# Early stage of a hybrid decoder block: x turned by TensorE, GpSimd left out, and emission ordered by model clocks

## The chip, the cores and the metric

One core of one Trainium2 chip. The metric is the device time of one execution in microseconds, the median of three runs.

## The reference

A residual block on x (512 tokens, 2048 channels, float32). What the early part of the kernel computes:

```python
mod = c @ w_ada[l] + b_ada[l]
shift, scale, gate = jnp.split(mod, 3, axis=-1)
h = rmsnorm(x, norm_gain[l]) * (1.0 + scale[:, None]) + shift[:, None]
proj = h @ w_in[l]
qa, ka, va, za, qm, km, vm, om, zm, ifg, ga, gb = jnp.split(proj, offsets, axis=-1)
...
qk = jax.nn.silu(causal_depthwise_conv(jnp.concatenate([qm, km], axis=-1), conv_w[l], conv_b[l]))
...
yb = (hm * jax.nn.silu(zm)) @ w_proj_mlstm[l]
```

The rest (dilated attention, the mLSTM in chunks, the merge, the output product, the last norm) comes later in the kernel and the change doesn't touch it.

## The kernel before, in words

All products are made in float32 by three fast products (`mm3`): each operand is split into a high part (a cast to fp32r on ScalarE, L172) and a low part (the difference, a subtraction, L173), and TensorE adds high x high, high x low, low x high.

The early stage makes sixteen blocks of h, transposed: h0 to h15, each 128 channels x 512 tokens, and with each of them the products that can be made already. One turn k consists of these steps:

- **Pieces.** The modulation c @ w_ada is made on VectorE, not on TensorE: a *piece* is a 128x1024 part of w_ada (transposed on the host) times c, summed along the row (`tensor_tensor_reduce`, L338). Scale and shift of a block need two pieces each, so a turn needs four, and the stage 64. The pieces lie in a ring `y` of eight buffers of 512 KB.
- **The chain of h.** When the fourth piece is done, `modulated(k)` (L391) makes gs (VectorE, 128x1, L393), modulates the block of x on ScalarE (L396), casts it (ScalarE, L172), makes the low part (VectorE for k = 0, otherwise GpSimd, L173), and stores h to DRAM.
- **First products.** A unit `ws[k]` (128x768) holds the weights of the six blocks of 128 columns in `FIRST`; its two halves make 9 matmuls each (`first_products`, L440), which accumulate in six PSUM banks over all k.
- **Extra products.** Ten more blocks of columns (`EXTRA`) are made in five groups of k (`GROUPS`: 2, 4, 4, 4 and 2 blocks of h). `TURNS` says which of them are emitted in which turn: a product is 3 matmuls for each block of its group, two products come from one unit of `wu`. Group 0 is copied to SBUF by ScalarE (L515), the others are added to it by VectorE (L517).

Weights come through a ring `raw` of three buffers and one `more`; high and low parts lie in rings `hi` and `lo` of four. A buffer is free again when the low part of its second half has been made. Low parts of `ws` are made by VectorE, those of the extra units by GpSimd. x comes transposed from the host (`xT`); it is squared on ScalarE, summed over channels by products with a matrix of ones, and each block is multiplied by the reciprocal root on GpSimd (`normed`, L387; the first on VectorE).

The order of instructions on each engine is the order in which the program emits them, and every engine works through its own in that order. All loads are emitted on SP's queue from one list `loads`, in the order in which units were added: `load_ahead` (L193) stops at the first whose ring has no free buffer. `step` (L256) keeps three split halves ahead (`prepare`, L207), emits what was left over (`late`), and then one product. How many pieces are emitted ahead of a product is a fixed count: `next_pieces` (L434) spreads the four pieces of turn k + 1 evenly over the products of turn k, two pieces ahead (`AHEAD`).

PSUM has five banks with tag `d` and three with tag `m`. After the early stage a stage of 258-column products over `wv` begins.

Of the kernel before, what the change touches and what calls it, by code (L numbers as in the profile page):

```python
# [11 lines left out]
F32 = mybir.dt.float32  # L12
# [39 lines left out]
TURNS = {  # L52
# [51 lines left out]
@with_exitstack  # L104
def block_kernel(ctx: ExitStack, tc, xT, x, c, cst, abias, ada, ws, wu, wv, fgain, out):
    nc = tc.nc
# [70 lines left out]
    pos = [0, 0]  # L177
    stream, loads, pieces, ready, late, tasks, beside = [], [], [], [], [], [], []
    at = {"load": 0, "split": 0, "half": 0, "piece": 0, "raw": 0, "more": 0, "y": 0}

# [8 lines left out]
    def add(u):  # L189
        stream.append(u)  # L190
        loads.append(u)

    def load_ahead():  # L193
        while at["load"] < len(loads):
            u = loads[at["load"]]
            if u.ring == "any":
                u.ring = "raw" if at["raw"] < RAW or "more" not in tags else "more"
            if at[u.ring] == {"raw": RAW, "more": MORE, "y": ADA}[u.ring]:
                if u.ring == "more":
                    u.ring = "any"  # L200
                break
            if u.at_load:
                u.at_load()
            u.raw = S(u.ring)
            dma(u.raw[:, : u.width], u.src)
            at["load"] += 1
            at[u.ring] += 1  # L207

    def prepare():

        if at["split"] == len(stream):
            return False
        load_ahead()
        u = stream[at["split"]]
        if at["half"] == 0 and u.at_split:
            u.at_split()
        if u.use:
            u.use(u.raw)
        else:
            n, i = u.width // 2, at["half"]  # L220
            if u.keep:
                hi, lo = u.keep()
            else:
                hi, lo = S("hi", F32R), S("lo", F32R)
            split(u.raw[:, i * n : (i + 1) * n], hi[:, :n], lo[:, :n], u.low)
            if later and u.low is None:
                normed(later.pop(0), nc.gpsimd)
            ready.append((u.products[i], hi, lo, u.keep is None))
# [18 lines left out]
    def modulate(n):  # L247

        while at["piece"] < min(n, len(pieces)):
            load_ahead()  # L250
            u = pieces[at["piece"]]
            u.use(u.raw)
            at["piece"] += 1
            at[u.ring] -= 1

    def step():  # L256
# [28 lines left out]
    cs = const.tile([P, C_MASK], F32, name="cs")  # L285
    xt = []

# [6 lines left out]

    def load_x(n):
        for _ in range(n):
            t = S("gm")
            dma(t, xT[len(xt)])
            xt.append(t)
# [4 lines left out]
    load_x(4)  # L304
# [4 lines left out]
    load_x(12)  # L309
    mask = S("mk")  # L310
# [6 lines left out]
    bmod = const.tile([P, 3 * KD], F32, name="bmod")  # L317
    nc.vector.tensor_copy(bmod, cs[:, C_BADA : C_BADA + 3 * KD])
    nc.vector.tensor_scalar(bmod[:, KD : 2 * KD], bmod[:, KD : 2 * KD], 1.0, None, ALU.add)
    cb = []  # L320
# [7 lines left out]
    def modulation(j, k, at_load=None, ring="any", then=None):  # L328

        col = j * KD + k  # L330
        acc = []

        def use(half):
            def f(raw):
                if half == 0:
                    acc.append(small([P, 1], "acc", 4))
                dst = acc[0] if half == 0 else mods[:, col : col + 1]
                nc.vector.tensor_tensor_reduce(  # L338
                    out=raw[:, :1024], in0=raw[:, :1024], in1=cb[half][:, :1024], scale=1.0,
                    scalar=bmod[:, col : col + 1] if half == 0 else acc[0],  # L340
                    op0=ALU.mult, op1=ALU.add, accum_out=dst,
                )
                if half and then:
                    then()
            return f

        for half in range(2):
            u = Unit(ada[col * 2 + half], use=use(half), at_load=at_load if half == 0 else None, ring=ring)
            loads.append(u)
            (pieces if then or ring == "y" else stream).append(u)  # L350
# [5 lines left out]
    qm, km, szm = [None] * 8, [None] * 8, [None] * 8  # L356

    def first_norm():

        acc = S("w")  # L360
# [11 lines left out]
        rstd = acc[:, 512:]  # L372
        nc.scalar.activation(rstd, ss, AF.Sqrt, bias=eps, scale=1.0 / D)
        nc.vector.reciprocal(rstd, rstd)
        rs.append(rstd)
        normed(0, nc.vector)
        modulate(3)
        for _ in range(2):
            prepare()
        modulate(4)  # L380
        for k in range(1, 4):
            normed(k, nc.gpsimd)

    rs = []
    later = []

    def normed(k, e):  # L387
        e.tensor_tensor(xt[k], xt[k], rs[0], ALU.mult)

    def modulated(k):  # L390
        def f():  # L391
# [12 lines left out]
            if k + 4 < KD:  # L404
                later.append(k + 4)
            hh.append(a)
# [23 lines left out]

    turn = []
    AHEAD = 2

    def next_pieces():  # L434

        k, n, i = turn
        modulate(4 * (k + 1) + AHEAD + 4 * (i + 1) // n)
        turn[2] += 1

    def first_products(k, half):  # L440
        def f(hi, lo):
            if half == 0:
                modulate(4 * (k + 1) + AHEAD)
                turn[:] = [k, 2 * (1 + len(TURNS.get(k, []))), 0]
# [7 lines left out]
            next_pieces()  # L452
        return f
# [50 lines left out]
    def extra_products(g, n):  # L504
        def f(hi, lo):
            ps = PS("m")
            k0, size = GROUPS[g]
            for kk in range(size):
                s = slice(kk * P, (kk + 1) * P)
                mm3(ps, hi[:, s], lo[:, s], hh[k0 + kk], hl[k0 + kk], kk == 0, kk == size - 1, True)  # L510

            def done():
                if g == 0:
                    extra.append(S("g"))
                    nc.scalar.copy(extra[n], ps)  # L515
                else:
                    nc.vector.tensor_tensor(extra[n], extra[n], ps, ALU.add)  # L517
# [3 lines left out]
            next_pieces()  # L521
        return f
# [3 lines left out]
    for k in range(KD):  # L526
        add(
            Unit(ws[k], 768, [first_products(k, 0), first_products(k, 1)], low=None)
        )
        modulation(1, k, ring="y")  # L530
        modulation(0, k, ring="y", then=modulated(k))
        for g, n in TURNS.get(k, []):
            width = 2 * GROUPS[g][1] * P
            add(
                Unit(next(src)[:, :width], width, [extra_products(g, n), extra_products(g, n + 1)], low=nc.gpsimd)
            )
    loads[:5] = loads[1:4] + loads[:1] + loads[4:5]
    load_ahead()
# [221 lines left out]
    def pair_units():  # L760

        for d in pairs():
            for u, src in enumerate(begin("S", d[2], d[3])):
                unit = Unit(src, ring="raw")
                loads.append(unit)
                paired.append((d, u, unit))
# [761 lines left out]
```

## Time and profile before

| what | value |
|---|---|
| runs, us | 1637.99, 1634.11, 1637.28 (median 1637.28) |
| profiled execution | 1637.23 us, span 1635.4 us |
| TensorE | 1565.2 us busy, 9686 matmuls |
| VectorE | 1147.9 us busy |
| ScalarE | 704.6 us busy |
| GpSimd | 139.8 us busy, nearly all before 260 us |
| DMA | 260.01 MB, mean 159 GB/s |

In the profile TensorE's matmuls are called PE (weight loads PEld), VectorE is DVE, ScalarE is ACT, GpSimd is POOL and the queue that issues the loads is SP. "L173" is line 173 of the program; since `split` is a helper, the names of the tiles tell whose low part it is. Times in a timeline count from the start of the span. The early stage runs from the start to about 247 us.

### The profile page before, as it was taken

How to read it: one execution, taken by the hardware profiler on the slowest of the kernel's cores; microseconds unless marked ns; L12 is line 12 of the kernel's file. 1: busy time of each engine (PE TensorE's matmuls, PEld its weight loads, DVE VectorE, ACT ScalarE, POOL GpSimd, SP SyncE). 2: the span in 40 equal slices, each digit the busy share in tenths (PEclk: the TensorE clock that was granted, in tenths of full speed). 3: DMA queues.
4: the chain of work that ended last, by engine and by line, in shares of the span. 5: the costliest groups of instructions: out<-in, count | busy, mean ns of one | idle time of the engine just before them, and what ended most of it. 6: DMA issues, size and time to landing. Idle time of an engine off the chain costs nothing.

```text
span 1635.4 us, 24961 instructions
## 1 busy us (share of the span) xinstructions
PE 1565.2 (96%) x9686; PEld 1388.3 (85%) x9686; DVE 1147.9 (70%) x1933; ACT 704.6 (43%) x1189; POOL 139.8 (9%) x112
## 2 busy tenths in 40 slices
PE   3799899999999999999999999999999999999997
PEld 1576689988888888999999999999999788878887
DVE  6788867667746568888788887888896444474445
ACT  3332344335525434455454454454443843343234
POOL 2665540000000000000000000000000000000000
PEclk7999999999999999999999999999999999999999
DMA  8677735665222344344443444444444654432333
GB/s 313 241 276 273 272 113 168 223 217 179 90 94 74 104 163 159 139 152 130 142 144 124 146 145 137 144 142 132 133 161 149 216 176 137 176 105 95 125 117 129
DMA packets 93879, 260.01 MB, mean 159 GB/s; under 512 B 10424, under 2 KB 14648, under 8 KB 93760
## 3 DMA queue, kind: packets, MB, share of 16 engines
q1 hardware_dynamic: 79928, 233.24, 41.6%
q10 hardware_dynamic: 13832, 25.18, 4.4%
q8 instruction: 76, 1.25, 0.3%
q14 instruction: 43, 0.35, 0.1%
HBM read 229.02 MB, written 29.36 MB: 158 GB/s over the span
## 4 chain that ended last, share of the span: by engine, by line
PE 71%; DVE 13%; issue 6%; ACT 4%; DMA 3%; POOL 1%; SPq 0%; ACTq 0%; DVEq 0%; POOLq 0%
PE ps L280 47%; PE ps L807 23%; DVE y L338 3%; DVE lo L173 2%; ACT sh L172 2%; DVE cs L780 1%; DVE e L822 1%; DVE cs L784 1%; DVE cs L785 1%; DMA raw<-ws 1%; DVE sl L173 1%; DVE al L786 1%; DMA p<-kept 1%; DMA more<-ws 1%; ACT gm L396 1%
## 5 line engine op out<-in xcount | busy, mean ns | idle before, releaser
L173 DVE TENSOR_TENSOR lo<-raw,hi 128x512 fp32r<-128x512 f32 (+2 forms) x238 | 177.5, 751 | 172.1 <-ACT hi L172 171.7
L172 ACT CAST hi<-raw 128x512 fp32r<-128x512 f32 (+3 forms) x276 | 161.2, 596 | 277.9 <-PE ps L280 227.4
L807 PE MATMUL ps<-t,sh 128*128 128x256 f32 x1344 | 245.3, 282 | 0.0
L807 PEld LDWEIGHTS ps<-t,sh 128*128 128x128 f32 x1344 | 208.0, 190 | 0.0
L807 PE MATMUL ps<-t,sl 128*128 128x256 f32 x672 | 189.3, 282 | 0.0
L779 ACT CAST ah<-raw 128x768 fp32r<-128x768 f32 x112 | 93.6, 836 | 204.8 <-issue 105.2
L280 PE MATMUL ps<-ha,hi 128*128 128x512 f32 x384 | 126.5, 409 | 26.1 <-ACT ha L172 17.2
L173 DVE TENSOR_TENSOR sl<-cs,sh 128x1024 fp32r<-128x1024 f32 x112 | 137.3, 1226 | 16.0 <-ACT sh L172 15.7
L172 ACT CAST sh<-cs 128x1024 fp32r<-128x1024 f32 x112 | 117.6, 1050 | 67.8 <-DVE cs L785 67.4
L786 DVE TENSOR_TENSOR al<-raw,ah 128x768 fp32r<-128x768 f32 x112 | 106.9, 955 | 52.8 <-ACT ah L779 52.6
L280 PE MATMUL ps<-hi,h 128*128 128x512 f32 (+1 forms) x512 | 143.6, 366 | 0.0
L280 PE MATMUL ps<-hi,ha 128*128 128x258 f32 (+1 forms) x512 | 129.8, 339 | 0.0
L280 PE MATMUL ps<-hi,hb 128*128 128x258 f32 (+1 forms) x512 | 129.3, 339 | 0.0
L807 PEld LDWEIGHTS ps<-t,sl 128*128 128x128 f32 x672 | 127.8, 190 | 0.0
L280 PE MATMUL ps<-hb,hi 128*128 128x512 f32 x384 | 122.0, 397 | 1.6 <-POOL hb L173 1.6
L280 PEld LDWEIGHTS ps<-ha,hi 128*128 128x128 f32 x384 | 73.9, 195 | 48.3 <-ACT ha L172 19.2
L280 PEld LDWEIGHTS ps<-hi,h 128*128 128x128 f32 x512 | 91.8, 188 | 17.0
L807 PE MATMUL ps<-hb,ah 128*128 128x256 f32 x448 | 87.1, 287 | 11.5 <-DVE e L822 9.9
L280 PEld LDWEIGHTS ps<-hi,ha 128*128 128x128 f32 x512 | 87.8, 188 | 11.4 <-issue 0.4
L280 PEld LDWEIGHTS ps<-hi,hb 128*128 128x128 f32 x512 | 87.9, 188 | 10.8
L280 PE MATMUL ps<-lo,h 128*128 128x512 f32 (+1 forms) x256 | 93.9, 367 | 2.4 <-DVE lo L173 2.4
L280 PE MATMUL ps<-h,hi 128*128 128x512 f32 x286 | 89.6, 395 | 0.0
(276 smaller groups left out, 3461.8 us busy)
## 6 DMA issues: line engine op xcount, KB each, us to landing
raw<-wu SPq DMA_DIRECT2D x223, 512.0 KB, 3.6
y<-ada SPq DMA_DIRECT2D x64, 512.0 KB, 7.3
g<-kept SPq DMA_DIRECT2D x56, 256.0 KB, 3.9
kept<-e ACTq DMA_DIRECT2D x56, 256.0 KB, 2.5
raw<-ada SPq DMA_DIRECT2D x24, 512.0 KB, 3.7
more<-wu SPq DMA_DIRECT2D x16, 512.0 KB, 3.5
raw<-wv SPq DMA_DIRECT2D x12, 516.0 KB, 3.7
kept<-g ACTq DMA_DIRECT2D x20, 256.0 KB, 4.2
```

What stands on the lines that cost most here:

```text
L172: nc.scalar.copy(hi, src)
L173: (low or nc.vector).tensor_tensor(lo, src, as32(hi), ALU.subtract)
L280: nc.tensor.matmul(ps, a, b, start=first and n == 0, stop=last and n == 2)
L338: nc.vector.tensor_tensor_reduce(out=raw[:, :1024], in0=raw[:, :1024], in1=cb[half][:, :1024], scale=1.0, scalar=bmod[:, col : col + 1] if ...
L396: nc.scalar.activation(xt[k], xt[k], AF.Identity, bias=mods[:, k : k + 1], scale=gs)
L779: nc.scalar.copy(ah, r[:, HT : 4 * HT])
L780: nc.vector.tensor_tensor(two(s[:, : 2 * HT]), two(r[:, HT : 3 * HT]), r[:, :HT].unsqueeze(1).to_broadcast([P, 2, HT]), ALU.add,)
L784: nc.vector.tensor_tensor(s[:, 2 * HT : 3 * HT], s[:, :HT], r[:, 2 * HT : 3 * HT], ALU.add)
L785: nc.vector.tensor_tensor(s[:, 3 * HT :], s[:, 2 * HT : 3 * HT], r[:, 3 * HT : 4 * HT], ALU.add)
L786: nc.vector.tensor_tensor(al, r[:, HT : 4 * HT], as32(ah), ALU.subtract)
L807: nc.tensor.matmul(banks[bank][:, n * HT : (n + 1) * HT], x[:, w], y, start=count[bank] == 1, stop=count[bank] == 24 * len(BANKS[bank]),)
L822: nc.vector.tensor_tensor(v[:, 0:2, :], twice(v[:, 4, :]), two(bb), ALU.add)
```

## The change

1. **x.** The host no longer transposes it. Sixteen tiles of 128 tokens x 512 channels are loaded from `x` (`load_x(j)`, four column parts j). Squares with an accumulator give the sums along the row, ten on ScalarE and six on VectorE; root and reciprocal are of 128x4 (one value for each token). `normed(j)` scales the four tiles of part j by a value for each partition, on ScalarE (half of part 0 on VectorE). `turned(k)` transposes a block by four 128x128 transposes of TensorE into an `m` bank, and ScalarE copies it to SBUF; blocks 0 and 1 stay in PSUM until they are modulated. Blocks 0 to 3 are turned ahead of the first product, 4 to 7 in turns 0 and 1, 8 to 15 behind the products of group 0.
2. **GpSimd.** All low parts of the stage are made by VectorE.
3. **Emission.** While pieces are left (`pacing`), the program keeps model clocks of SP, DMA, ScalarE, VectorE and TensorE with fixed prices for each operation. Loads stand in two lists (`y` and `raw`), and the next load is taken from the list whose buffer is free first by these clocks. A low part is `owe`d: it is emitted (`settle`) when VectorE's model clock has passed its cast, or when the product that needs it is next. `fill` emits pieces as long as they end before a time that is worked out for the next cast or 4 us before the next product is due. `AHEAD` and `next_pieces` are gone.
4. **TURNS.** All five units of group 0 are in turn 1 (before: turns 1 to 4).

The core of the diff:

```diff
-    1: [(0, 0)], 2: [(0, 2), (0, 4)], 3: [(0, 6)], 4: [(0, 8)],
+    1: [(0, 0), (0, 2), (0, 4), (0, 6), (0, 8)],
...
+        while pacing() and not (want and want.raw is not None):
+            kinds = []
+            for kind in loads:
+                if loads[kind]:
+                    ring = loads[kind][0].ring
+                    rings = ["y"] if ring == "y" else ["raw", "more"]
+                    times = [free[r][0] for r in rings if free[r]]
+                    if times:
+                        kinds.append((min(times), kind))
+            if not kinds or (not want and min(kinds)[0] > clock["DVE"]):
...
+            if not begin_load(min(kinds)[1]):
+                break
...
+    BEGIN, LAND, LOAD = 0.45, 2.0, 1.3 / 1024
+    PIECE, CHAIN, CAST, LOW, MATMUL = 1.33, 1.65, (0.13, 0.00096), (0.15, 0.00105), 0.233
+    room = {"raw": RAW, "more": MORE, "y": ADA}
...
+    def settle(until=None):
+        while owed and (owed[0][0] <= clock["DVE"] if until is None else until in [o[1] for o in owed]):
+            t, key, cost, f = owed.pop(0)
+            clock["DVE"] = max(clock["DVE"], t) + cost
+            ready_at[key] = clock["DVE"]
+            f()
...
+    def fill(until):
+        while at["piece"] < len(pieces):
+            load_ahead()
+            settle()
+            u = pieces[at["piece"]]
+            if at["piece"] % 4 == 3 and at["piece"] // 4 not in xt:
+                break
+            if u.raw is None or max(clock["DVE"], u.there) + PIECE > until + 0.4:
+                break
+            modulate(at["piece"] + 1)
...
+        if pacing():
+            load_ahead(u)
+            n = u.width // 2
+            cast = lambda: max(clock["ACT"], ends[at["half"] + 2 * at["split"]], u.there) + CAST[0] + CAST[1] * n
+            due = clock["PE"] + sum(3 * MATMUL / P * r[4][2] for r in ready if r[4])
+            come = max(ends[at["half"] + 2 * at["split"]], u.there) + CAST[0] + CAST[1] * n
+            fill(max(come, due - 4.0))
...
+            clock["ACT"] = cast()
+            nc.scalar.copy(hi[:, :n], part)
+            def low():
+                nc.vector.tensor_tensor(lo[:, :n], part, as32(hi[:, :n]), ALU.subtract)
+                if i == 1:
+                    at[u.ring] -= 1
+                    free[u.ring].append(clock["DVE"])
...
+            owe(clock["ACT"], (u, i, n), LOW[0] + LOW[1] * n, low)
+            ready.append((u.products[i], hi, lo, True, (u, i, n)))
+            at["half"] = 1 - i
...
         pending, late[:] = list(late), []
         for f in pending:
+            fill(clock["PE"])
             f()
-        f, hi, lo, _ = ready.pop(0)
+        f, hi, lo, _, key = ready.pop(0)
+        if key:
+            settle(key)
+            clock["PE"] = max(clock["PE"], ready_at.get(key, 0.0))
         f(hi, lo)
+        if key:
+            ends.append(clock["PE"])
         pump()
...
-        ss = PS("m")
-        for k in range(KD):
-            sq = acc[:, :512] if k == 0 else S("hb")
-            nc.scalar.activation(sq, xt[k], AF.Square)
-            if k % 3 == 2 and k < KD - 2:
-                nc.tensor.matmul(ss, ones, sq, start=k == 2, stop=False)
-            elif k:
-                nc.vector.tensor_tensor(acc[:, :512], acc[:, :512], sq, ALU.add)
-        nc.tensor.matmul(ss, ones, acc[:, :512], start=False, stop=True)
...
+        for j in range(NT):
+            for t in range(NT):
+                to, junk = sums[:, t, j : j + 1], S("hb")
+                if (j * NT + t) % 8 in (2, 5, 7):
+                    nc.vector.tensor_tensor_reduce(
+                        out=junk, in0=xn[j][t], in1=xn[j][t], scale=1.0, scalar=0.0,
+                        op0=ALU.mult, op1=ALU.add, accum_out=to,
+                    )
+                else:
+                    nc.scalar.activation(junk, xn[j][t], AF.Square, accum_out=to)
...
+        nc.vector.tensor_reduce(rstd, sums, mybir.AxisListType.X, ALU.add)
+        nc.scalar.activation(rstd, rstd, AF.Sqrt, bias=eps, scale=1.0 / D)
         nc.vector.reciprocal(rstd, rstd)
...
+        normed(0, True)
+        for k in (2, 3, 0, 1):
+            turned(k)
+        clock["DVE"] = clock["ACT"] = clock["PE"] = clock["DMA"] = 5.0
+        normed(1)
         for _ in range(2):
             prepare()
         modulate(4)
...
+    def normed(j, both=False):
+        for t in range(NT):
+            r = rstd[:, t : t + 1]
+            clock["ACT"] += 0.0 if both else 0.62
+            if both and t % 2:
+                nc.vector.tensor_scalar(xn[j][t], xn[j][t], r, None, ALU.mult)
+            else:
+                nc.scalar.activation(xn[j][t], xn[j][t], AF.Copy, scale=r)
+    def turned(k):
+        ps = PS("m")
+        clock["PE"] += 0.5
+        end = clock["PE"]
+        for t in range(NT):
+            nc.tensor.transpose(ps[:, t * P : (t + 1) * P], xn[k // 4][t][:, k % 4 * P : (k % 4 + 1) * P], ident)
+        def copy():
+            xt[k] = S("hb" if k < HK else "gm")
+            clock["ACT"] = max(clock["ACT"], end) + 0.55
+            nc.scalar.copy(xt[k], ps)
+        if k < 2:
+            xt[k] = ps
+        elif k < 4:
+            copy()
+        else:
+            late.append(copy)
...
-            nc.scalar.activation(xt[k], xt[k], AF.Identity, bias=mods[:, k : k + 1], scale=gs)
+            src = xt[k]
+            if k < 2:
+                xt[k] = S("hb")
+            nc.scalar.activation(xt[k], src, AF.Identity, bias=mods[:, k : k + 1], scale=gs)
...
-            split(xt[k], a, b, nc.gpsimd if k else None)
+            nc.scalar.copy(a, xt[k])
+            clock["DVE"] += 0.15
+            clock["ACT"] = max(clock["ACT"], clock["DVE"]) + CHAIN
+            owe(clock["ACT"], k, 0.7, lambda: nc.vector.tensor_tensor(b, xt[k], as32(a), ALU.subtract))
             put(("h", k), xt[k])
...
+                modulate(4 * (k + 1))
+                settle(k)
+                clock["PE"] = max(clock["PE"], ready_at[k])
...
+            clock["PE"] += 9 * MATMUL
+            for j in {(0, 0): (4, 5), (1, 0): (6,), (1, 1): (7,)}.get((k, half), ()):
+                turned(j)
+            if (k, half) == (1, 1):
+                normed(2)
...
+            clock["PE"] += 3 * size * MATMUL
+            end = clock["PE"]
+            if g == 0 and n < 8:
+                turned(8 + n)
+            if g == 0 and n == 1:
+                normed(3)
```

## Rows read from the trace of the kernel before

**Rows 1.** Page, busy time, share of the span, instructions of each engine.
```profile
PE 1565.2 (96%) x9686; PEld 1388.3 (85%) x9686; DVE 1147.9 (70%) x1933; ACT 704.6 (43%) x1189; POOL 139.8 (9%) x112
```
**Rows 2.** Windows of TensorE, line 280: stretch, busy (matmuls), granted clock, DMA share, GB/s.
```profile
0.00:36.07 36.07, 0.00 (x1) 0.74 0.88 328
36.07:194.78 158.71, 138.97 (x546) 0.96 0.73 261
194.78:240.00 45.22, 45.22 (x194) 1.00 0.43 151
...
36.07:41.23 5.16, 5.16 (x12) 0.50 0.52 188
```
**Rows 3.** Chain of waits up to 300 us, its last piece: start, length, what.
```profile
194.78 105.31 PE ps L280 x665
```
**Rows 4.** Timeline, the first matmul of the next stage: start, length, engine, operation.
```profile
246.77 0.28 PE L280 MATMUL ps<-hi,ha 128*128 128x258 f32 x1
```
**Rows 5.** Timeline from the squares to the end of the fourth piece.
```profile
8.54 8.03 ACT L366 ACTIVATE hb<-gm 128x512 f32<-128x512 f32 x12 [0.74 <-DMA gm<-xT]
...
20.55 3.35 DVE L374 RECIPROCAL w<-w 128x512 f32<-128x512 f32 x1 [2.89 <-ACT w L373]
...
24.55 2.29 DVE L338 CUSTOM_DVE_ANT_0 y<-y,w,bmod 128x1024 f32<-128x1024 f32 x1
...
34.37 0.08 DVE L338 DVE_READ_ACCUMULATOR2_ANT mods<- 128x1 f32 x1
```
**Rows 6.** The tiles of x: durations, first and last issue; time to landing.
```profile
L154 SPq DMA_DIRECT2D gm<-xT x16: 327/399/549, 0.7 to 10.5; - x16
...
DMA to landing us min/median/max: 2.9/5.2/5.5
```
**Rows 7.** Timeline of VectorE and GpSimd around 37 us; in brackets GpSimd's idle time.
```profile
36.66 0.55 DVE L173 TENSOR_TENSOR lo<-raw,hi 128x384 fp32r<-128x384 f32 x1
37.12 1.28 DVE L338 CUSTOM_DVE_ANT_0 y<-y,w,bmod 128x1024 f32<-128x1024 f32 x1
...
42.20 0.15 DVE L393 TENSOR_TENSOR gs<-mods,cs 128x1 f32<-128x1 f32 x1
...
43.99 1.27 POOL L173 TENSOR_TENSOR ha<-gm,ha 128x512 fp32r<-128x512 f32 x1 [11.63 <-ACT ha L172]
```
**Rows 8.** Groups of VectorE up to 240 us: count, busy, mean ns, idle before.
```profile
L338 DVE CUSTOM_DVE_ANT_0 y<-y,w,bmod 128x1024 f32<-128x1024 f32 x32 | 59.2, 1850 | 0.0
L338 DVE CUSTOM_DVE_ANT_0 y<-y,w,acc 128x1024 f32<-128x1024 f32 x32 | 47.7, 1489 | 0.7
L173 DVE TENSOR_TENSOR lo<-raw,hi 128x384 fp32r<-128x384 f32 x24 | 31.1, 1302 | 22.1 <-ACT hi L172 22.1
L517 DVE TENSOR_TENSOR g<-g,ps 128x512 f32<-128x512 f32 x34 | 23.0, 678 | 11.0 <-PE ps L280 11.0
```
**Rows 9.** Groups of VectorE from 240 to 600 us.
```profile
L173 DVE TENSOR_TENSOR lo<-raw,hi 128x512 fp32r<-128x512 f32 x63 | 43.0, 688 | 36.8 <-ACT hi L172 36.7
...
L173 DVE TENSOR_TENSOR y<-y,y 128x258 fp32r<-128x258 f32 x16 | 5.7, 422 | 0.0
```
**Rows 10.** Windows, busy PE, PEld, DVE, ACT, POOL; clock, DMA share, GB/s.
```profile
60.00:80.00 20.00, 16.23 (x65) 12.14 (x64) 15.25 (x20) 9.16 (x19) 11.86 (x9) 0.97 0.86 304
...
140.00:160.00 20.00, 18.55 (x78) 14.63 (x79) 18.09 (x24) 5.16 (x9) 15.93 (x9) 1.00 0.77 259
...
36.07:194.78 158.71, 138.97 (x546) 104.70 (x546) 132.08 (x165) 50.47 (x95) 92.19 (x57) 0.96 0.73 261
```
**Rows 11.** Timeline, four transposes in a stream of matmuls later on.
```profile
424.23 0.39 PE L280 MATMUL ps<-hb,lo 128*128 128x512 f32 x1
...
424.46 0.60 PE L982 MATMUL ps<-cs,w 128*128 128x128 f32 x4
...
424.81 0.71 PE L280 MATMUL ps<-hb,hi 128*128 128x512 f32 x2
```
**Rows 12.** Waits from 36.07 to 194.78: total, times, longest.
```profile
DVE lo L173 <- ACT hi L172: 26.1, 13, 2.7
```
**Rows 13.** Waits of SP's queue, the same stretch.
```profile
SPq L154 <- DVE lo L173: 91.4, 13, 9.7
```

More of the change, by code (lines that the diff above doesn't have):

```diff
@@ L177, in block_kernel @@
     pos = [0, 0]
-    stream, loads, pieces, ready, late, tasks, beside = [], [], [], [], [], [], []
-    at = {"load": 0, "split": 0, "half": 0, "piece": 0, "raw": 0, "more": 0, "y": 0}
+    stream, loads, pieces, ready, late, tasks, beside = [], {"y": [], "raw": []}, [], [], [], [], []
+    at = {"split": 0, "half": 0, "piece": 0, "raw": 0, "more": 0, "y": 0}
     def begin(*desc):
@@ L190, in add @@
         stream.append(u)
[L191 to L200, printed above, removed]
-                break
[L202 to L207, printed above, removed]
+        loads["raw"].append(u)
@@ new lines, in begin_load @@
+    def begin_load(kind):
+        u = loads[kind][0]
+        if u.ring == "any":
+            u.ring = "raw" if at["raw"] < RAW or "more" not in tags else "more"
+        if at[u.ring] == room[u.ring]:
+            if u.ring == "more":
+                u.ring = "any"
+            return False
+        if u.at_load:
+            u.at_load()
+        u.raw = S(u.ring)
+        dma(u.raw[:, : u.width], u.src)
+        loads[kind].pop(0)
+        at[u.ring] += 1
+        if pacing():
+            clock["SP"] = max(clock["SP"], free[u.ring].pop(0)) + BEGIN
+            clock["DMA"] = max(clock["DMA"], clock["SP"] + LAND) + LOAD * u.width
+            u.there = clock["DMA"]
+        return True
@@ new lines, in load_ahead @@
+    def load_ahead(want=None):
+        while pacing() and not (want and want.raw is not None):
[8 more added lines that the diff above has]
+            if not kinds or (not want and min(kinds)[0] > clock["DVE"]):
+                break
+            if not begin_load(min(kinds)[1]):
+                break
+        if not pacing():
+            for kind in loads:
+                while loads[kind] and begin_load(kind):
+                    pass
@@ new lines, in block_kernel, with pacing @@
+    BEGIN, LAND, LOAD = 0.45, 2.0, 1.3 / 1024
+    PIECE, CHAIN, CAST, LOW, MATMUL = 1.33, 1.65, (0.13, 0.00096), (0.15, 0.00105), 0.233
+    room = {"raw": RAW, "more": MORE, "y": ADA}
+    free = {r: [0.0] * n for r, n in room.items()}
+    clock = {"SP": 0.0, "DMA": 0.0, "ACT": 0.0, "DVE": 0.0, "PE": 0.0}
+    owed, ends, ready_at = [], [0.0] * SPLIT, {}
+    def pacing():
+        return at["piece"] < len(pieces)
+    def settle(until=None):
[4 more added lines that the diff above has]
+            f()
@@ L212, in prepare @@
             return False
+        u = stream[at["split"]]
         load_ahead()
-        u = stream[at["split"]]
+        if pacing():
+            load_ahead(u)
[4 more added lines that the diff above has]
+            fill(max(come, due - 4.0))
+            hi, lo = S("hi", F32R), S("lo", F32R)
+            i = at["half"]
+            part = u.raw[:, i * n : (i + 1) * n]
+            clock["ACT"] = cast()
[8 more added lines that the diff above has]
+            at["half"] = 1 - i
+            if i == 1:
+                at["split"] += 1
+            return True
         if at["half"] == 0 and u.at_split:
@@ L225, in prepare @@
             split(u.raw[:, i * n : (i + 1) * n], hi[:, :n], lo[:, :n], u.low)
-            if later and u.low is None:
-                normed(later.pop(0), nc.gpsimd)
-            ready.append((u.products[i], hi, lo, u.keep is None))
+            ready.append((u.products[i], hi, lo, u.keep is None, None))
             at["half"] = 1 - i
@@ L249, in modulate @@
         while at["piece"] < min(n, len(pieces)):
-            load_ahead()
             u = pieces[at["piece"]]
+            load_ahead(u)
+            settle()
+            clock["DVE"] = max(clock["DVE"], u.there) + PIECE
             u.use(u.raw)
@@ L254, in modulate @@
             at[u.ring] -= 1
+            free[u.ring].append(clock["DVE"])
+            load_ahead()
     def step():
@@ L285, in block_kernel @@
     cs = const.tile([P, C_MASK], F32, name="cs")
-    xt = []
+    xt = {}
     begin_psum(5, 3)
@@ L293, in block_kernel, with load_x @@
     begin_part("heads", "left", y=(8, 1032), w=(4, 1024), gm=(17, 512), mk=(1, P))
[L295 to L299, printed above, removed]
+    xn = [[None] * NT for _ in range(NT)]
+    def load_x(j):
+        for t in range(NT):
+            xn[j][t] = S("gm")
+            dma(xn[j][t], x[t * P : (t + 1) * P, j * T : (j + 1) * T])
     crow = [S("g") for _ in range(4)]
@@ L308, in block_kernel @@
     tri = cs[:, C_TRI : C_TRI + P]
-    load_x(12)
+    for j in range(1, NT):
+        load_x(j)
     mask = S("mk")
@@ L348, in modulation @@
             u = Unit(ada[col * 2 + half], use=use(half), at_load=at_load if half == 0 else None, ring=ring)
-            loads.append(u)
+            loads["y" if ring == "y" else "raw"].append(u)
             (pieces if then or ring == "y" else stream).append(u)
@@ L380, in first_norm @@
         modulate(4)
[L381 to L388, printed above, removed]
+    def normed(j, both=False):
[10 more added lines that the diff above has]
+        end = clock["PE"]
+        for t in range(NT):
+            nc.tensor.transpose(ps[:, t * P : (t + 1) * P], xn[k // 4][t][:, k % 4 * P : (k % 4 + 1) * P], ident)
[9 more added lines that the diff above has]
+            late.append(copy)
     def modulated(k):
@@ L514, in done @@
                     extra.append(S("g"))
+                    clock["ACT"] = max(clock["ACT"], end) + 0.6
                     nc.scalar.copy(extra[n], ps)
                 else:
+                    clock["DVE"] = max(clock["DVE"], end) + 0.62
                     nc.vector.tensor_tensor(extra[n], extra[n], ps, ALU.add)
@@ L520, in f @@
             late.append(done)
-            next_pieces()
         return f
@@ L527, in block_kernel @@
         add(
-            Unit(ws[k], 768, [first_products(k, 0), first_products(k, 1)], low=None)
+            Unit(ws[k], 768, [first_products(k, 0), first_products(k, 1)])
         )
@@ L534, in block_kernel @@
             add(
-                Unit(next(src)[:, :width], width, [extra_products(g, n), extra_products(g, n + 1)], low=nc.gpsimd)
+                Unit(next(src)[:, :width], width, [extra_products(g, n), extra_products(g, n + 1)])
             )
-    loads[:5] = loads[1:4] + loads[:1] + loads[4:5]
+    for kind, n in (("y", 4), ("raw", 1), ("y", 4), ("raw", 1)):
+        for _ in range(n):
+            begin_load(kind)
     load_ahead()
@@ L764, in pair_units @@
                 unit = Unit(src, ring="raw")
-                loads.append(unit)
+                loads["raw"].append(unit)
                 paired.append((d, u, unit))
```

33 lines of the change are left out of this document (10 added, 23 removed).

## The prediction

> **What bounds the kernel now.** I read the shares of the engines first, then TensorE's stretches, then the chain of waits. TensorE is busy 96% of the span [rows 1], so only what it loses can be won. The windows show where: the early stage has 768 matmuls of 512 columns, the first starts at 36.07 us, 546 of them take the 158.71 us up to 194.78, and the last 222 run unbroken until the next stage's first matmul at 246.77 [rows 2, 4]. In the unbroken stretch a matmul takes 45.22 / 194 = 0.233 us; 768 of them are 178.9. The stage takes 246.77 - 36.07 = 210.7, so it loses 31.8 us behind its first matmul, and 36.07 ahead of it. The chain says the same: from 194.78 on it is one piece of TensorE, well into the next stage [rows 3]; ahead of that it goes through modulation pieces, low parts and activations. After the stage the change alters nothing. **The working is therefore one number: when the early stage ends on TensorE; what it ends sooner than 246.77 is won.** The profiled execution took 1637.23 us, its span 1635.4, and the median of the runs is 1637.28, so a gain is taken from 1637.3 directly.
>
> **Part 1, the start.** Before, the squares on ScalarE end at 16.57, the ones product of TensorE and the root on ScalarE follow, then a reciprocal of 128x512 on VectorE, which starts its first piece at 24.55; the fourth is done at 34.37, GpSimd multiplying beside them [rows 5]; the first matmul comes 1.7 us later, at 36.07. After, tokens lie on partitions, so the sum of squares is an accumulator of each square, and root and reciprocal are of 128x4. The loads of x are as many and as large, the last issued at 10.5 and landing 5.2 later, 15.7 [rows 6]. From there: one 512-wide reduce on VectorE, a shape I have no row for; half a piece is 0.64 [rows 7] and a low part of 512 is 0.69 [rows 9]; with the accumulator read I take 0.75. The two bmod ops, the reduce, the root and the reciprocal are small, some 0.2 each with their hops: 1.2. Two scalings on ScalarE at the price of the squares, 12 in 8.03 [rows 5]: 1.3. VectorE's first piece comes at 15.7 + 0.75 + 1.2 + 1.3 = 19.0; with a hop, **19.2**. Four pieces at 1.28 without GpSimd [rows 7] are 5.1, then gs and 1.7 as before: first product at 19.2 + 5.1 + 0.35 + 1.7 = **26.4**. The transposes of four blocks, two copies, four scalings and two casts, some 6 us of ScalarE, lie beside the four pieces. Bounds: 24.5 (the small ops all hidden) and 30 (ScalarE's row of small jobs reaches past the pieces and delays the chain by 3.6).
>
> **Part 2, VectorE without GpSimd.** Beside GpSimd the 64 pieces take 1.85 and 1.49 us in the mean and the low parts of 384 take 1.30 [rows 8]; around 37 us, where GpSimd waits, the same two take 1.28 and 0.55 [rows 7]. The additions that read PSUM take 0.68 beside GpSimd [rows 8], no more than a low part of that width takes in the later stages without it [rows 9]. So what GpSimd slows is the op with both inputs in SBUF, and its removal gives back 106.9 - 81.9 = 25 us on pieces and 32 x 0.75 = 24 on low parts. What VectorE takes over: 15 low parts of h and 30 of 512 at 0.69, 20 of 256 at 0.42 [rows 9]: 10.4 + 20.7 + 8.4 = 39.5. GpSimd's 15 multiplications become 14 scalings on ScalarE and 2 on VectorE; ScalarE gains these and 14 copies, at 0.67 some 19 us in a stage where it is busy 50.47 of 158.71 [rows 10].
>
> VectorE's work from 19.2 until the low part of h15, the last that TensorE must wait for: 64 pieces x 1.28 = 81.9; 30 low parts of ws x 0.55 = 16.5; 16 of h x 0.69 = 11; 16 gs x 0.15 = 2.4; group 0, 10 x 0.42 = 4.2; groups 1 and 2, 20 x (0.69 + 0.68) = 27.4; the 6 products of group 3 ahead of turn 15, 6 x 1.37 = 8.2; with 1.5 for the first chain's gap, **153 us**. Without idle time h15 stands at 172. Behind it TensorE has 18 + 48 + 60 = 126 matmuls, 29.4 us.
>
> **Part 3, TensorE.** New are 16 turned blocks of four transposes. In a running stream later in the trace four such transposes put 0.58 between the starts of two matmuls instead of 0.23, and the pair behind takes 0.71 where 0.62 is usual: 0.44 a block [rows 11]. Twelve come behind the first product: 5.3 us; the ones products that go were ahead of it. The Trainium skill (TensorE: Matmul & The Clock Gate, Part 4: PE-mode transpose) gives about 275 ns for one transpose in a kernel; 48 of them one behind the other would be an estimated 13 us, 8 us less gain; the rows show overlap, four in 0.60. The clock: the first 12 matmuls ran at 1.2 GHz (granted 0.50), after TensorE had stood idle, and took 5.16 us where 2.8 is the fast price [rows 2]; these 2.4 us I count again. One PSUM bank holds h1's block until h1 is modulated, and block 5, which needs it, is transposed between the two halves of turn 0: TensorE's queue, the second half with it, waits there for h1's activation, 2 us (bounds 0 and 4, the 18 matmuls of a turn). In turn 1 one `m` bank belongs to the first products, and the extra products and turned blocks alternate in the other two: product n + 1 waits for the copy of product n, 0.67 and a hop, with 0.44 of transposes ahead of it, so about 0.35 ten times, 3.5 (bounds 0 and 8: ScalarE has some 25 us of copies, casts, scalings and chains there, TensorE 23, and more if a chain holds the copies up). If TensorE never waited otherwise, the stage would end at 26.4 + 178.9 + 5.3 + 2.4 + 2 + 3.5 = **218.5**.
>
> **Part 4, the order.** TURNS now puts all of group 0 into turn 1: 78 matmuls there, 18 us, in which VectorE (7.1 a turn and 4.2 for the group) gets ahead. Then it has turns 2 to 4, 4.2 us of TensorE each against its 7.1, which eat that lead; from turn 5 on the two are near balance (four turns: 192 matmuls, 44.7 us, against 4 x 7.1 + 13.7 = 42). TensorE reaches h15 at 218.5 - 29.4 = 189.1, so VectorE has to be busy 153 / (189.1 - 19.2) = 90% of the time not to be late. In the old order it was busy 132.08 of 158.71, 83%, and 90% in its best stretch [rows 10]: it stood in front of low parts whose cast was not done, 26.1 us in 13 waits [rows 12]. The new order emits a low part when its model clock has passed the cast, and fills with pieces until then; between 83 and 100 I take 90, which the old order reached for 20 us: h15 at 19.2 + 153 / 0.90 = 189.2, the stage's end at **218.6**, both engines in step. At its tail a product of group 4 costs VectorE 1.1 us and one op of 512 for the convolutions beside it, about 0.7,, against 1.4 of TensorE, for some seven products: 3 us late, less what is prepared ahead; I take 1 (bounds 0 and 3). End at 219.6, gain 27: **1610 us**.
> The loads: up to h15 the program needs 33.6 MB of pieces, 6.3 of ws, 8.1 of group weights, 4.5 of x and constants, and writes 3.9 back, 56.4 MB. By 26.4 some 8.7 are through, at the 328 GB/s of the start [rows 2]; 47.7 MB in 189 - 26 us is 293 GB/s. The stage ran at 261 and at 304 in a good stretch [rows 10]. It is enough, without much room. SP's queue stood 91.4 us of the stage in front of buffers that VectorE's low parts free [rows 13]; two load lists, taken by which buffer frees first, should shorten that.
>
> **Rivals.** (a) *The order is no better.* VectorE is busy 83% as before, because its model clocks drift from the real ones: h15 at 19.2 + 153 / 0.83 = 203.5, end 233, gain 14, 1623; at 80% the gain is 7. For it: one queue now carries all, and each wait holds everything behind it. Against: 90% was reached even beside GpSimd. (b) *Loads become the bound, and it is slower.* All low parts are now VectorE's, emitted late (about 4 us before their due time) behind pieces; the four weight buffers stay held until the second low part, SP stands at the next weight, and the pieces behind it don't start. At the old 261 GB/s h15 comes at 26.4 + 47.7 / 0.261 = 209, end 238.5, 1629. The point from which it decides against the change is 47.7 / (246.8 - 29.4 - 26.4) = 250 GB/s; at 240 the end is 254.6 and the time 1645. Against it: pieces free their eight buffers without a low part, and the choice between the lists avoids a held buffer. (c) *VectorE is not relieved.* If the 1.85 and 1.30 have another cause (the loads, say), the work is 106.9 + 41.7 and some 53 for the rest, 202 us, and the end 19.2 + 202 / 0.90 + 29.4 = 273: 1663. The clean rows speak against it. (d) *All goes right*: no bank waits, VectorE never late: 213, 1603.5; with the start at its lower bound 1601.6.
>
> **How the numbers follow.** About 0.3%, 5 us, can be told from no change here. Forecast and (d), gains of 20 to 35: 0.64. (a), gains of 5 to 20: 0.22. Between 5 us faster and 5 slower, (b) near its point of decision: 0.06. (b) beyond it 0.06, (c) 0.02. So faster 0.86, same 0.06, slower 0.08. The range takes in (d)'s lower end, 1602, and (a) down to 80%, 1630.
>
> **What would show it.** Pieces at 1.28 and low parts of 384 at 0.55 (part 2); the stage's first product near 26.4 (part 1); idle time of TensorE mainly in turns 0 and 1 (part 3); VectorE busy about 90% from 20 to 190, loads at 290 GB/s there, the next stage's first matmul near 220 (part 4). The prediction is wrong if VectorE still stands in front of casts, if SP's waits for low parts hold the pieces, or if ScalarE's copies of turned blocks, which wait for TensorE in its queue, hold an h behind them.

## The result and the profile after

The changed kernel takes 1616.91 us (median of 4 runs, 1616.09 to 1617.62), the kernel before 1635.69 in the same comparison: ratio 0.9885, 95% interval 0.9867 to 0.9903, **18.8 us faster**. The prediction was 1610 in a range of 1602 to 1630. The profiled executions are 21.1 us apart (1637.23 and 1616.09), since that of before lies at the upper end of its runs; their spans are 1635.4 and 1613.8.

The number that the prediction worked out is where the next stage begins on TensorE. Timeline of the kernel after, first matmul of the early stage and first of the next:

```profile
26.39 0.79 PE L375 MATMUL ps<-ha,hi 128*128 128x512 f32 x1 [3.82 <-ACT ha L529]
...
223.64 0.28 PE L375 MATMUL ps<-hi,ha 128*128 128x258 f32 x1
```

Before they stood at 36.07 and 246.77 [rows 2, 4]: 23.1 us of stage end won, where 27 were forecast. Windows of TensorE (stretch, busy, granted clock, DMA share, GB/s) and the last pieces of the chain of waits up to 300 us show where the rest of the loss sits:

```profile
26.39:32.53 6.14, 5.80 (x17) 0.51 1.00 384
32.53:64.49 31.96, 24.56 (x119) 1.00 0.96 362
...
64.49:223.64 159.15, 159.15 (x685) 1.00 0.66 241
```
```profile
63.85 0.59 ACT gm L505
64.44 0.04 issue
64.49 235.54 PE ps L375 x1317
```

From 64.49 on TensorE isn't idle for a moment; before, that began at 194.78 [rows 3]. What is lost behind the first product lies in turns 0 and 1. One period of turn 1 in the timeline:

```profile
52.13 0.60 PE L501 MATMUL ps<-cs,gm 128*128 128x128 f32 x4
...
52.76 0.58 ACT L505 COPY gm<-ps 128x512 f32<-128x512 f32 x1
...
53.24 0.59 ACT L647 COPY g<-ps 128x512 f32<-128x512 f32 x1
...
53.40 0.73 PE L375 MATMUL ps<-ha,hi 128*128 128x512 f32 x2 [0.67 <-ACT gm L505]
```

TensorE transposes the next block, ScalarE copies *that* first (L505) and the finished product second (L647), and the next product starts the moment the first copy is done: it gets the turned block's bank. The period is 2.77 us (from 53.40 to the next such start at 56.17), against 6 x 0.233 + 0.45 = 1.85 without waits.

Groups of VectorE up to 240 us (count, busy, mean ns, idle before), to be laid beside [rows 8]:

```profile
L434 DVE CUSTOM_DVE_ANT_0 y<-y,w,acc 128x1024 f32<-128x1024 f32 x32 | 41.0, 1280 | 2.0 <-DMA y<-ada 1.6
L434 DVE CUSTOM_DVE_ANT_0 y<-y,w,bmod 128x1024 f32<-128x1024 f32 x32 | 40.9, 1279 | 0.0
L650 DVE TENSOR_TENSOR g<-g,ps 128x512 f32<-128x512 f32 x40 | 27.4, 684 | 23.2 <-PE ps L375 23.2
L291 DVE TENSOR_TENSOR lo<-raw,hi 128x384 fp32r<-128x384 f32 x22 | 11.9, 552 | 3.0 <-ACT hi L288 3.0
```

1.28 and 0.55, to the hundredth what the rows of idle GpSimd had said. And VectorE's window from its first piece to the low part of h15 (busy, instructions, clock, DMA share, GB/s), and all engines from 26 to 152 us, after and then before:

```profile
19.00:173.20 154.20, 132.93 (x242) 0.98 0.88 328
```
```profile
26.00:152.00 126.00, 117.88 (x509) 93.36 (x510) 108.03 (x197) 58.70 (x108) 0.11 (x1) 0.97 0.95 353
```
```profile
26.00:152.00 126.00, 100.31 (x387) 75.36 (x388) 104.20 (x131) 39.16 (x75) 72.87 (x45) 0.91 0.72 258
```

The DMA engines moved 353 GB/s, busy 95% of the time; before, 258 GB/s and 72%. The prediction would have been wrong if VectorE still stood in front of casts. Its waits for casts from 19 to 190 us (total, times, longest) are, after:

```profile
DVE lo L291 <- ACT hi L288: 6.2, 8, 1.5
DVE lo L173 <- ACT hi L172: 3.9, 4, 1.5
DVE ha L532 <- ACT ha L529: 3.5, 2, 2.7
```

That is 13.6 us; before, the same stretch has 27.6 (26.1 of them the waits of [rows 12]).

### The profile page after: what moved, and what is told of

It is laid out like the page before. It is cut to its first block, busy times and chain, and to the rows that moved or that the text cites. A ratio compares the mean times of both kernels' runs of the same rounds, so it can differ in the third digit from the quotient of the medians.

```text
span 1613.8 us, 25094 instructions
## 1 busy us (share of the span) xinstructions
PE 1564.0 (97%) x9740; PEld 1398.9 (87%) x9740; DVE 1126.6 (70%) x2001; ACT 719.0 (45%) x1221; POOL 17.3 (1%) x32
## 4 chain that ended last, share of the span: by engine, by line
PE 84%; DVE 6%; ACT 4%; issue 2%; DMA 2%; SPq 0%; ACTq 0%; DVEq 0%
PE ps L375 55%; PE ps L941 29%; ACT sh L172 1%; DMA gm<-x 1%; DVE lo L173 1%; DVE e L956 1%; DMA p<-kept 1%; DVE cs L914 1%; DVE sl L173 1%; ACT gm L493 1%; DVE h L173 0%; DVE cs L918 0%; PE ps L501 0%; PE ps L1241 0%; DVE cs L919 0%
## 5 line engine op out<-in xcount | busy, mean ns | idle before, releaser
L173 DVE TENSOR_TENSOR lo<-raw,hi 128x512 fp32r<-128x512 f32 (+2 forms) x231 | 155.6, 678 | 153.8 <-ACT hi L172 153.4
L172 ACT CAST hi<-raw 128x512 fp32r<-128x512 f32 (+2 forms) x231 | 139.6, 610 | 273.3 <-PE ps L375 214.1
```

Source lines behind the costliest of these rows:

```text
L172: nc.scalar.copy(hi, src)
L173: (low or nc.vector).tensor_tensor(lo, src, as32(hi), ALU.subtract)
```

## The experiments

All were compared with the kernel before on the same chip, where its median was 1634.5 to 1636.3. The stage end (first matmul of the next stage) is the measure, since what follows varies by itself: from the stage end to the end of the span it took 1388.6 us before, 1390.2 after, and 1390.0 to 1393.5 in the experiments. A stage end comes from one profiled execution, while the runs of a changed kernel (4 to 10) spread over 0.2 to 3.9 us, those of e5 over 9.9; a difference of about 2 us between stage ends needs a row of the trace beside it.

| kernel | first product | stage end | median us | ratio to before |
|---|---|---|---|---|
| before | 36.07 | 246.77 | 1635.69 | |
| after | 26.39 | 223.64 | 1616.91 | 0.9885 |
| e5: before, without GpSimd | 31.94 | 240.12 | 1628.31 | 0.9955 (0.994 to 0.997) |
| e6: after, fixed order | 32.28 | 239.66 | 1634.37 | 0.9996 (0.9986 to 1.0006) |
| e12: after, pieces fixed, low parts by clocks | 26.63 | 229.04 | 1624.59 | 0.9933 (0.9918 to 0.9948) |
| e11: after, low parts at once, pieces by clocks | 28.63 | 250.95 | 1643.72 | 1.0047 (1.0032 to 1.0062) |
| e10: after, one load list | 26.36 | 243.78 | 1636.08 | 0.9995 (0.9986 to 1.0005) |
| e4: after, GpSimd makes extra low parts | 26.07 | 225.43 | 1617.75 | 0.9898 (0.9883 to 0.9913) |
| e1: after, product's copy first | 26.02 | 221.38 | 1614.26 | 0.9866 (0.9852 to 0.9881) |
| e2: after, turned copies on VectorE | 25.89 | 228.91 | 1622.28 | 0.9918 (0.9901 to 0.9935) |
| e8: e1 and e2 | 26.84 | 230.00 | 1622.13 | 0.9915 (0.9901 to 0.993) |
| e3: after, old TURNS | 26.57 | 221.44 | 1615.80 | 0.9874 (0.9859 to 0.9889) |
| e9: e1 and e3 | 26.04 | 219.86 | 1613.32 | 0.9861 (0.9847 to 0.9876) |

**Which part carries the gain: GpSimd, or the order?** e5 takes GpSimd out of the kernel before and nothing else:

```diff
-                normed(later.pop(0), nc.gpsimd)
+                normed(later.pop(0), nc.vector)
...
-            split(xt[k], a, b, nc.gpsimd if k else None)
+            split(xt[k], a, b)
...
-[extra_products(g, n), extra_products(g, n + 1)], low=nc.gpsimd)
+[extra_products(g, n), extra_products(g, n + 1)])
```

> The kernel before with GpSimd's work (low parts of extra units and of h, multiplications by the root) given to VectorE; x, the fixed order and TURNS as before. Theory: pieces at 1.28 and low parts of 384 at 0.55, so VectorE's sum stays about even (49 us back, 50 added), the start gains about 3 us (pieces 5 instead of 10, one multiplication more) and the fixed order still leaves VectorE in front of casts: the stage ends at 236 to 246 instead of 246.77. Rival (the removal of GpSimd alone is the gain): 226 to 232.

6.7 us of stage end, 4.1 of them ahead of the first product: the theory's range, and far from the rival. The profiled execution is the slowest of e5's eight (1632.35); between medians the gain is 6.2 us. VectorE now stands 23.0 us in front of casts of h (15 waits from 31.9 to 193.7 us). e4 goes the other way, `(u.low or nc.vector).tensor_tensor(lo ...)` with `low=nc.gpsimd` on the extra units:

> The changed kernel, but the low parts of the extra units are made by GpSimd again (those of ws and h stay on VectorE; the model clocks go on as if VectorE made them). Theory of the prediction: GpSimd slows VectorE's ops with two SBUF inputs, so pieces go from 1.28 to 1.5 to 1.7 us in the mean and low parts of 384 to about 1.0; VectorE loses about as much as it hands over, and TensorE waits for GpSimd's own low parts (1.8 us each against 0.69): the stage ends 3 to 12 us later, 227 to 236. Rival: with an order that fits, GpSimd costs nothing: 223 to 225.

```profile
L434 DVE CUSTOM_DVE_ANT_0 y<-y,w,acc 128x1024 f32<-128x1024 f32 x32 | 47.5, 1484 | 2.5 <-DMA y<-ada 1.8
...
L650 DVE TENSOR_TENSOR g<-g,ps 128x512 f32<-128x512 f32 x40 | 26.9, 681 | 29.1 <-PE ps L375 28.9
```
```profile
PE ps L375 <- POOL lo L291: 1.9, 1, 1.9
```

The pieces do slow down (1.48 and 1.43), additions that read PSUM don't (0.681), yet the stage ends only 1.8 us later, below the theory's range, and in time e4 can't be told from the change (the intervals overlap). VectorE is busy 138.62 us in the stretch where it was busy 132.93, and TensorE waits for none of it: its waits from 20 to 230 us are those of the change and the one in the second fence, for a low part that GpSimd itself makes late. The mechanism of part 2 is there; under this order, and with half of GpSimd's former work (46.04 us of 154.20, before 92.19 of 158.71 [rows 10]), VectorE's slack takes it up. The Trainium skill (GPSIMD Engine Reference, Key points) says that GpSimd shares its SBUF interfaces with VectorE, with contention for ops in a 2-port mode or with two SBUF inputs; the two rows agree with it.

e6 keeps x turned, no GpSimd, the load lists and the new TURNS, and puts the old rule of the order back: `owe` emits the low part at once, `fill` emits no piece, `next_pieces` with `AHEAD = 2` does.

> The changed kernel (x turned, no GpSimd, load lists and TURNS new) with the old rule for the order on VectorE: a low part is emitted right behind its cast, and pieces by a fixed count (AHEAD 2, spread evenly over the products of a turn). Theory of the prediction: VectorE stands in front of casts, TensorE waits in many turns, the stage ends at 230 to 238 instead of 223.64. Rival: the order by clocks brings nothing beyond a faster VectorE: 223 to 226.

All of the gain is gone from the time, and 16.0 us from the stage end (of the 7.1 that stay, the rest of the kernel took back 3.8). Even the first product comes 5.9 us later. The timeline of VectorE in e6 shows why:

```profile
18.01 0.88 DVE L484 TENSOR_SCALAR gm<-gm,rstd 128x512 f32<-128x512 f32 x2
24.45 1.03 DVE L284 TENSOR_TENSOR lo<-raw,hi 128x384 fp32r<-128x384 f32 x2 [5.55 <-ACT hi L281]
25.39 1.28 DVE L427 CUSTOM_DVE_ANT_0 y<-y,w,bmod 128x1024 f32<-128x1024 f32 x1
```

Two low parts stand in front of the first four pieces and wait 5.55 us for a cast that is queued on ScalarE behind copies and scalings; the change began these pieces at 18.98. So the shorter start of part 1 hangs on the order too: with low parts held back alone (e12) the first product comes at 26.63, with pieces by clocks alone (e11) at 28.63. Under the old order the turned x brings next to nothing: e6 and e5, which differ in x, the lists and `TURNS`, end the stage at 239.66 and 240.12, and in time e6 is the slower (1634.37 against 1628.31). What turning x is worth under the new order no run shows.

**Which half of the order?** e11 changes `owe` alone (the low part at once), e12 the pieces alone (fixed count):

> The changed kernel, but every low part is emitted on VectorE right behind its cast (pieces are still filled in by the model clocks). It splits the 16 us that the fixed order costs (stage end 239.66 instead of 223.64). Theory of the prediction: VectorE standing in front of casts is the loss; then most of it comes back here, the stage ends at 232 to 240. Rival (the number and time of the pieces is what counts): 224 to 228.

> The other half: low parts are held back by the model clocks as in the change, but pieces are emitted by the old fixed count (two ahead, spread evenly over the products of a turn). Theory (low parts in front of casts are the loss): the stage ends at 224 to 229. Rival (pieces): 233 to 240, since TensorE waits at the first products of turns for an h whose pieces were spread over products instead of done as soon as they were loaded.

Holding low parts back is the larger half: with fixed pieces it brings 239.66 to 229.04, at the edge of the theory's range, with filled pieces 250.95 to 223.64. VectorE's waits for casts from 19 to 190 us go the same way: 42.8 us in e6, 48.0 in e11, 18.3 in e12, 13.6 in the change. e11 is slower than the kernel before (1.0047), which neither theory of it gave. Its waits from 19 to 195 us (total, times, longest) fit a ring:

```profile
ACT hi L289 <- PE ps L376: 38.2, 19, 3.8
DVE lo L292 <- ACT hi L289: 28.0, 13, 4.7
...
PE ps L376 <- ACT ha L530: 18.9, 6, 5.8
```

(The longest of the last, 5.8, is that ahead of the first product.) A cast waits until a product of TensorE frees one of the four `hi` buffers; the low part waits for the cast, and with it the pieces behind it on VectorE; the next h then comes late, and TensorE, which would free the buffer, waits for h. Filling in pieces by clocks without holding low parts back is worse than not filling (250.95 against 239.66).

**The loads.** e10 takes loads in the order in which units were added:

```diff
-                    if times:
-                        kinds.append((min(times), kind))
+                    kinds.append((loads[kind][0].serial, kind, times))
```

A weight at the list's head then blocks the pieces; where a unit or a piece isn't loaded when it is due, pieces or low parts ahead of it are emitted first.

> The changed kernel with loads in the order in which the units were added (one list, the head of which blocks the rest), as before the change; emission by clocks otherwise. The prediction held that two lists shorten SP's waits and that at 250 GB/s the loads would decide. Theory: pieces come later, loads fall from 352 GB/s between 26 and 152 us to about 290 to 320, TensorE waits for some h: the stage ends at 226 to 234. Rival (loads lead by so much that their order is free): 223 to 225.

20.1 us later, beyond the theory's range: the lists are as necessary as the held low parts. SP's waits from 26 to 152 us, of after and then of e10, and e10's window of the same stretch:

```profile
SPq L154 <- DVE lo L291: 7.8, 11, 1.4
```
```profile
SPq L155 <- DVE lo L296: 78.8, 17, 11.8
```
```profile
26.00:152.00 126.00, 107.57 (x434) 81.92 (x435) 83.68 (x153) 49.62 (x93) 0.00 (x0) 0.96 0.70 259
```

259 GB/s instead of 353, as before the change. VectorE waits 9.2 us for loads of pieces (19 to 190 us), in the change 1.6. This is rival (b) of the prediction, made to happen: low parts that come late hold weight buffers, and a single list passes that on to the pieces. Part of e10's loss may come from pieces emitted ahead of their time to get at a load; the two weren't separated.

**Turn 1.** e1 moves `turned(8 + n)` behind `late.append(done)`, so that the product's copy goes first:

> The changed kernel with one thing moved: behind a product of group 0 its own copy to SBUF is emitted first and the turned block behind it, where the change emits the turned block and its copy first. Theory: turn 1 of the changed kernel loses 0.92 us a product (period 2.77 us for six matmuls and four transposes, 1.85 without waits) because the next product gets the bank that the turned block held and waits for its copy, which can't start before the transposes end; with the product's copy first, that copy runs beside the transposes, the period falls to about 2.35, eight times, and the early stage ends 3 to 4 us sooner, at about 220 instead of 223.64. Rival: ScalarE is simply full in turn 1 (copies, casts, scalings, chains); then the order of two copies changes nothing, 223 to 224.

The wait of a middle period falls from 0.67 to 0.24 and the period from 2.77 to 2.33. The stage ends 2.3 us sooner (0.4 of that from the first product), less than expected, since the first two waits (1.50 and 1.64) stay and two later ones are 0.54 and 0.64: there ScalarE's own row of scalings and the chain of h hold the copy up. Both causes are there; the order of banks is the larger. In time the intervals of e1 and the change overlap; it is the period that shows the effect.

> The changed kernel with the copies of turned blocks 8 to 15 made by VectorE. Theory (order of the banks): the next product still waits for the turned block's copy, now 0.68 us on VectorE and sometimes behind a piece of 1.28, so the period stays at 2.7 or more, the stage ends at 223 to 228. Rival (ScalarE is full): eight copies of 0.58 and their waits leave ScalarE, the stage ends 4 to 6 us sooner, 218 to 220.

> Both of these: the product's copy first on ScalarE, the turned block's copy on VectorE. Theory: the two copies run side by side, the period comes near 2.1 to 2.35, the stage ends at 218 to 220, the time 4 to 6 us below the changed kernel. Rival (VectorE, waiting for transposes in its queue, delays the pieces and the next h): no better than the changed kernel.

In e2 neither theory held: the period fell to 2.33, and yet the stage ended at 228.91. In e8 the rival held. With the copies on VectorE turn 1 does run faster (in e2 the ninth of its ten extra products starts at 59.45 instead of 64.49, and the first two waits are 0.78 each), so ScalarE's share was real. But the stage ends 5.3 and 6.4 us later. Waits of e2 from 40 to 110 us:

```profile
DVE gm L506 <- PE ps L501: 7.6, 6, 2.2
...
PE ps L375 <- ACT ha L533: 5.0, 2, 3.8
```

VectorE stands 7.6 us in front of transposes, the pieces behind it come late, and TensorE pays at h of the next turns. By the program, TensorE's model clock knows no waits for banks, so it can let a copy through as if TensorE were on time.

> The changed kernel with the old TURNS (group 0 spread over turns 1 to 4). The prediction said that all of group 0 in turn 1 lets VectorE get ahead for turns 2 to 4. If that lead is needed, TensorE waits for h2 to h5 and the stage ends 5 to 10 us later, 229 to 234. If it isn't (VectorE had h15 ready 20 us before TensorE came to it), the end stays within 2 us of 223.64, or comes sooner since first products between the extra ones cover copies.

The lead that part 4 valued isn't needed: with the old TURNS TensorE waits for no h behind 40 us, and the stage ends 2.2 us sooner, as first products between the extra ones leave fewer waits for copies (5 instead of 8). In time e3 can't be told from the change: 1615.80, the intervals overlap, and the profiled execution is its fastest.

> The changed kernel with the product's copy first (as in e1) and the old TURNS (as in e3). If the two gains (2.3 and 2.2 us of stage end) come from different waits they add: five waits of 0.67 in e3 become about 0.24, stage end at 219 to 220, the time about 1612. If both removed the same wait, 221 to 222.

The two gains add in the main: 219.86, and 1613.32 us is the fastest kernel of the study, 3.6 us below the change (the intervals of the two ratios overlap at their edges).

## Why the prediction came out as it did

- **Part 1, the start**: right, and the hundredth is luck. First product forecast 26.4, measured 26.39; VectorE's first piece 19.2, measured 18.98. The last tile of x landed at 16.50, not 15.7, and the small steps behind it took 2.5 us where 3.5 were priced; ScalarE's casts then held h0's modulation from 24.30 to 24.91. Not foreseen: that the start needs the new order (e6 32.28).
- **Part 2, prices**: right, 1.28 and 0.55. **Its sum**: mis-sized. 153 us was a sum of durations; VectorE was busy 132.93 us in that stretch. About 11 us of the difference is overlap: an op's row begins before that of the op ahead of it ends, by 0.07 to 0.09 us in 141 cases. The rows of before show it already: a low part of 0.55 begins at 36.66 and the piece behind it at 37.12 [rows 7]. The other 9 us are work that the sum had put ahead of h15 and that came behind it, mainly of group 3, and the 1.5 us of gap.
- **Part 3, TensorE**: right in kind, too small. Up to 64.49 the 84 matmuls, twelve blocks, slow clock and both bank waits were to take 32.8 us and took 38.1. The clock was at 0.51 until 32.53, as assumed. The bank wait of turn 0, put at 2 us, did not come: the eight transposes of blocks 4 and 5 ran in one piece, and the second half of turn 0 behind them, before ScalarE read h1's block out of its bank, so block 5 did not need that bank:

```profile
31.09 1.68 PE L501 MATMUL ps<-cs,gm 128*128 128x128 f32 x8
...
32.53 0.71 PE L375 MATMUL ps<-ha,hi 128*128 128x512 f32 x2
...
33.29 0.79 ACT L523 ACTIVATE hb<-ps,mods,gs 128x512 f32<-128x512 f32 x1
```

The waits of turn 1, put at 3.5 us, cost 9.3: from 40.35, where the first product of group 0 starts, to 64.49 are 24.1 us against 8 x 1.85. A wait for a copy was put at 0.35 a product; the period lost 0.92 in the middle (0.67 of it TensorE idle) and 1.9 at the first two, since the wait was taken for the product's own copy, with the transposes ahead of it, and is for the copy of the turned block, behind them (e1).
- **Part 4, the order**: the direction right, the bound wrong. 90% of 153 us put h15 at 189.2, in step with TensorE; its low part was begun at 172.51, while TensorE came to it at 223.64 - 29.3 = 194.3. VectorE was busy 86% only, since it had less to do than 153 us, and not late after turn 1: the two were not in step. That TURNS gives a needed lead fell with e3. The tail's 1 us didn't come.
- **The loads**: 293 GB/s were held to be enough without much room; they ran at 353, well above the 304 that the prediction had taken as a good stretch. The condition of rival (b), a weight that blocks the pieces, is what the two lists take away; e10 shows it, at 259 near the rate of before.
- **The sum**: 27.2 us forecast; turns 0 and 1 took 5.3 more, the tail 1.0 and the matmuls 0.2 less: 23.1 of stage end. The rest of the span took 1.5 more and what lies around the span 0.5, 21.1 between the profiled executions; between medians 18.8. Why what follows the stage is longer wasn't settled; the experiments show it too, so it is hardly this kernel's own. 18.8 us lies in the band of gains (5 to 20) that the prediction had given (a) and a chance of 0.22, but not by (a)'s mechanism.
- **Rivals**: (a) fell: VectorE's busy share, 86%, is near (a)'s 83, but h15 came at 172.5 and not at 203.5. (c) fell to the pieces' 1.28. What no rival named is that the parts need each other: GpSimd's removal alone is worth 6.7 us of stage end, with x turned, the lists and TURNS but the old order it is 7.1, and with the order by clocks 23.1.

## What to carry to other kernels

On an engine that works in order, put behind whatever can run now what waits for another engine, and check the ring that such a wait closes (buffer, cast, low part, piece, h, product): half of a scheduling change can be worse than none. Loads whose buffers come free by different work (here pieces and weights) belong in separate lists, so that one kind doesn't block the other. To find an engine's load, add starts to starts from a dense stretch, not durations; and of two copies that free banks, emit first the one whose data is ready first.

## What the runs showed of the hardware

- The rows of back-to-back VectorE ops overlap by 0.07 to 0.09 us. From 19.00 to 173.20 the 242 durations of the changed kernel add up to 149.2 us where the engine was busy 132.93; 5.2 us are 64 short accumulator reads.
- The DMA engines held 353 GB/s at a share of 0.95 for 126 us, with products, pieces and stores going on (the changed kernel, 26 to 152 us).
- Four transposes of 128x128 between matmuls put 0.45 us between the end of the matmul ahead and their own end (49.50 to 49.95 in the chain of waits of the changed kernel); their row lasts 0.60 from its start at 49.34, beside that matmul.
